# Reciprocal roots of latent and token-block norms taken by GpSimd's power in place of eleven small VectorE operations

## The chip, the cores and the metric

The kernel is one program on one core of a Trainium2 chip. Its engines are TensorE (PE, matrix products; PEld is its loading of the stationary operand), VectorE (DVE), ScalarE (ACT), GpSimd (POOL) and SyncE (SP, which issues the transfers). Each engine works through its own instructions in program order and waits at an instruction until what that instruction needs is there. The metric is device time in microseconds (us).

## The reference, cut to what matters

Two layers of a hybrid encoder over 1024 tokens of width 1024, in f32. Each layer has a token mixer of four head groups (a convolution module, a gated linear recurrence, a short gated convolution and latent attention), then cross-attention into 256 memory tokens, then a SwiGLU feed-forward part. The change touches the latent attention alone:

```python
def rms_norm(x, g):
    y = x * lax.rsqrt(jnp.mean(x * x, axis=-1, keepdims=True) + EPS)
    return y * g

def mla(ud, cos, sin, qa_g, wuq, kva_g, wukv, qn_g, kn_g):
    cq, ckv, kr = jnp.split(ud, [256, 384], axis=-1)
    q  = (rms_norm(cq, qa_g) @ wuq).reshape(b, s, 4, 96)
    kv = (rms_norm(ckv, kva_g) @ wukv).reshape(b, s, 4, 128)
    k_nope, v = jnp.split(kv, [64], axis=-1)
    k = concatenate([k_nope, broadcast_to(kr, (b, s, 4, 32))], axis=-1)
    q, k = rms_norm(q, qn_g), rms_norm(k, kn_g)
    # rotary on the last 32 of 96 columns of q and k
    return blocked_attention(q, k, v)
```

So every token has two latent norms (`cq` of 256, `ckv` of 128 columns) and eight head norms (four of `q`, four of `k`, 96 columns each), and each needs a reciprocal square root.

## The kernel before, in words

**Products.** f32 operands are split into a high and a low part, and a product is three matmuls (high by high, high by low, low by high: `mm3`). A product of a weight tile with 512 tokens is 24 matmuls, `pd<-n,wh` twice for each `pd<-n,wl`, where `n` is the normed input in 128-row pieces, and `wh`, `wl` are the parts of a weight that arrives by DMA as `wr`, is copied by ACT (L136) and has its remainder taken by DVE or POOL (L137). Results stand in three kinds of PSUM buffers, two of each: `pd`, the "t" kind (`cs`, `ukv`, `uq`, `rb`), and one for scores.

**Latent attention.** `mla_proj` makes the three latent pieces `ch`, `cl` (high and low part) and their squares `sqv`, `sqq`. `mla_stats` (once for each latent norm) sums the squares of the eight token blocks with TensorE (`cs<-ones,sq`, 128x1 each), multiplies twice by the norm of the layer's input (`xr`), takes the reciprocal roots of eight columns and leaves them in `rqkv`. `mla_prep` works on a pair of token blocks of 128, so four calls a layer. For each block it makes `ukv` (three matmuls of 512 columns), evicts keys and values by ACT, takes the low part `V` by DVE (L659), sums the squares of the keys (L662), then makes `uq` (six matmuls of 384 columns), copies it and sums its squares (L669). Of the pair's sixteen sums `hss` it takes the reciprocal roots `hr`; these scale `tok`, the queries and keys (L685 and L686 on DVE, L687 on POOL), and the rotary part follows on DVE and POOL (L696 to L698).

`ukv`, `uq`, `cs` and the transposes `hT` of the keys share the two "t" buffers. TensorE can make the `uq` of a block only when the buffer of the `ukv` before it is free, and that is after L659.

**The roots.** `rsqrt_cols` scales and adds epsilon (L147, `ra`). It then has two ways. Without the flag, POOL raises to the power -0.5 in one operation (L149):

```python
        if not act:
            nc.gpsimd.tensor_tensor(out=out, in0=a, in1=self.nhalf[:, :n], op=ALU.pow)
            return
```

With the flag, DVE takes a first guess by a shift and a subtraction on the bits (L152, L153) and makes three Newton steps of three operations (L155 to L157): eleven operations, each on `n` columns.

**Order.** The mixer (`block`) calls its parts by a written list of tokens, `ORDER`; `mt` is `mla_stats`, `pr` is `mla_prep`, `mp` the latent products, `cx`, `ct` and `sb` the short convolution (`cpad`, `yc`, `gc`), `hk` and `hh` the transposes of keys and queries, `S` the first scores. `PRIO` gives some of them a head start, `pr.0` one of 1200. A scheduler then places the instructions of each engine by these and by its own estimates of durations, so another operation in `rsqrt_cols` also changes where its neighbours stand.

The part of the list around the change, once per layer:

```
uk ih.1.0 mp.0 kr mp.2 po.0 nd po.1 mt.0 mp.1 rg mt.1 pr.0 fl.0
cx.0 pr.1 cx.1 ct.1 ct.0 fl.1 sb.0 hk.0.0 pr.2 pr.3 sb.1 hk.0.1 hh.0.0 hh.0.1 S.0
```

Of the kernel before, what the change touches and what calls it, by code (L numbers as in the profile page):

```python
# [79 lines left out]
class Trunk:  # L80
# [542 lines left out]
    def mla_stats(self, i, sq, rq):  # L623
        nc = self.nc
        p = self.pt("cs")
        for b in range(8):
            self.mm(p[:, b:b + 1], sq[i][:, b * 128:(b + 1) * 128], self.ones[:, 0:1])
        a = self.st("rqa")
        rr = rq[:, 8 * i:8 * i + 8]
        for hf in range(2):  # L630
            r1, o = self.r1[hf][:, :4], hf * 4
            nc.vector.tensor_tensor(out=a[:, o:o + 4], in0=p[:, o:o + 4], in1=r1, op=ALU.mult)
            nc.vector.tensor_tensor(out=a[:, o:o + 4], in0=a[:, o:o + 4], in1=r1, op=ALU.mult)
        self.rsqrt_cols(a[:, :8], 8, (128, 256)[i], rr, True)
        for hf in range(2):
            o = hf * 4
            nc.vector.tensor_tensor(out=rr[:, o:o + 4], in0=rr[:, o:o + 4], in1=self.r1[hf][:, :4], op=ALU.mult)

    def mla_prep(self, B0, cq, rq, ks, rt, wuq, wukv, tok, V):
        nc = self.nc  # L640
        tok += [self.m4("tok") for _ in range(2)]
        V.append(self.m4("V", F32R))
        i96 = 96 ** -0.5
        ss = self.st("hss")
        ssv = ss[:, :16].rearrange("p (b j) -> p b j", b=2)
        for b in range(2):
            B = B0 + b
            o = B * 128
            q4 = tok[B][:, 0:384].rearrange("p (h e) -> p h e", h=4)
            k4 = tok[B][:, 384:768].rearrange("p (h e) -> p h e", h=4)  # L650
            p2 = self.pt("ukv")
            self.mm3(p2, [(cq[2][0][:, o:o + 128], cq[2][1][:, o:o + 128], wukv[0][:, :512], wukv[1][:, :512])])
            rk = rq[:, B:B + 1]
            pk = p2[:, :256].rearrange("p (h e) -> p h e", h=4)
            nc.scalar.activation(out=k4[:, :, 0:64], in_=pk, func=AF.Identity, scale=rk)
            Vv = V[B // 2][:, (B % 2) * 512:(B % 2) * 512 + 512].rearrange("p (h j e) -> p h j e", h=4, j=2)
            pv = p2[:, 256:512].rearrange("p (h e) -> p h e", h=4)
            nc.scalar.activation(out=Vv[:, :, 0, :], in_=pv, func=AF.Identity, scale=rk)
            nc.vector.scalar_tensor_tensor(out=Vv[:, :, 1, :], in0=pv, scalar=rk, in1=Vv[:, :, 0, :].bitcast(F32), op0=ALU.mult, op1=ALU.subtract)  # L659
            s = self.t2("hk")  # L660
            nc.scalar.activation(out=s[:, :256].rearrange("p (h e) -> p h e", h=4), in_=k4[:, :, 0:64], func=AF.Square, scale=i96)
            nc.vector.tensor_reduce(out=ssv[:, b, 4:8], in_=s[:, :256].rearrange("p (h e) -> p h e", h=4), op=ALU.add, axis=AX.X)  # L662
            p = self.pt("uq")
            self.mm3(p[:, :384], [(cq[k][0][:, o:o + 128], cq[k][1][:, o:o + 128],
                                   wuq[0][:, k * 384:(k + 1) * 384], wuq[1][:, k * 384:(k + 1) * 384]) for k in range(2)])
            nc.scalar.copy(out=tok[B][:, 0:384], in_=p[:, :384])
            s = self.t2("hq")
            nc.scalar.activation(out=s[:, :384], in_=tok[B][:, 0:384], func=AF.Square, scale=i96)
            nc.vector.tensor_reduce(out=ssv[:, b, 0:4], in_=s[:, :384].rearrange("p (h e) -> p h e", h=4), op=ALU.add, axis=AX.X)  # L669
        nc.vector.tensor_tensor(out=ssv[:, :, 4:8], in0=ssv[:, :, 4:8], in1=ks[:, B0:B0 + 2].unsqueeze(2).to_broadcast([128, 2, 4]), op=ALU.add)  # L670
        rqb = rq[:, 8 + B0:10 + B0].unsqueeze(2).to_broadcast([128, 2, 4])
        for _ in range(2):
            nc.vector.tensor_tensor(out=ssv[:, :, 0:4], in0=ssv[:, :, 0:4], in1=rqb, op=ALU.mult)
        r = self.st("hr")
        self.rsqrt_cols(ss[:, :16], 16, 1, r[:, :16], True)
        rv = r[:, :16].rearrange("p (b j) -> p b j", b=2)
        nc.vector.tensor_tensor(out=rv[:, :, 0:4], in0=rv[:, :, 0:4], in1=rqb, op=ALU.mult)
        for b in range(2):
            self.mla_rope(B0 + b, tok, rv[:, b, :], rt)
# [815 lines left out]
```

## Time and profile before

| | |
|---|---|
| timed, median of 3 | 2930.03 us (2922.39 to 2930.04) |
| profiled execution | 2921.93 us, span 2920.2 us, mean granted clock 0.974 |
| TensorE | 2769.6 us busy, 14520 matmuls |
| VectorE | 1844.2 us busy, 2793 instructions |
| GpSimd | 1266.6 us busy, 845 instructions |
| ScalarE | 1095.2 us busy, 1826 instructions |

The span is the time from the first instruction to the last on the profiled core; the profiled execution's own time is 1.7 us more. A timeline line gives the start and the duration of one instruction (or a run of equal ones, xcount), its engine, line and tiles (out<-in, without the numbers of the tiles); the bracket at its end is the idle time of that engine just before it and the instruction that ended it. DVE operations overlap their neighbours a little, so starts can be closer together than durations.

### The profile page before, as it was taken

To read this page: it belongs to the slowest core of one execution; us is meant where nothing else is said; L and a number is where in the kernel's file an instruction comes from. 1 tells how busy PE (TensorE), PEld (TensorE's weight loads), DVE (VectorE), ACT (ScalarE), POOL (GpSimd) and SP (SyncE) were. 2 spreads that over 40 slices of the span, in tenths; PEclk is the share of its full clock that TensorE was granted. 3 is DMA by queue.
4 is the path that set the end of the run, shared out by engine and by line. 5 is a ranking of instruction groups with operands and counts; after the bars stand their busy time and mean duration, and the time that the engine had idled before them with its cause. 6 is when DMAs were issued, how large, how long until landed. Compare 5 with 4: busy or idle time off the path is not lost.

```text
span 2920.2 us, 37768 instructions
## 1 busy us (share of the span) xinstructions
PE 2769.6 (95%) x14520; PEld 2299.1 (79%) x14520; DVE 1844.2 (63%) x2793; ACT 1095.2 (38%) x1826; POOL 1266.6 (43%) x845
## 2 busy tenths in 40 slices
PE   8979999998899999999999899999998999999999
PEld 6868878887678888777878687788776788887877
DVE  7986778576745555553359767785766455556332
ACT  5314427454532222431233244274554322224111
POOL 4122214242467777434331232242334687774422
PEclk9989999998999999999999999999989999999999
DMA  4200111230212222434221001112202222224423
GB/s 143 67 28 26 44 54 35 94 94 15 84 56 85 87 87 87 141 128 136 73 101 42 17 26 51 56 57 76 80 25 84 65 87 79 75 85 163 129 76 101
DMA packets 85572, 222.00 MB, mean 76 GB/s; under 512 B 9744, under 2 KB 9872, under 8 KB 85392
## 3 DMA queue, kind: packets, MB, share of 16 engines
q1 hardware_dynamic: 84240, 215.40, 23.1%
q0 software_dynamic: 1152, 4.19, 0.5%
q8 instruction: 114, 1.87, 0.3%
q14 instruction: 66, 0.54, 0.1%
HBM read 173.42 MB, written 46.14 MB: 75 GB/s over the span
## 4 chain that ended last, share of the span: by engine, by line
PE 67%; DVE 14%; issue 7%; POOL 5%; ACT 4%; DMA 2%; SPq 0%; DVEq 0%; POOLq 0%; ACTq 0%
PE pd L119 29%; PE X L119 7%; PE Q L119 7%; PE R L119 7%; PE Y L119 4%; DVE cacc L545 3%; PE pv L119 2%; PE S L119 2%; PE PT L749 2%; PE lv L119 1%; DMA hr<-h_scr 1%; PE cs L119 1%; PE rb L119 1%; DVE n L808 1%; DVE AT L410 1%
## 5 line engine op out<-in xcount | busy, mean ns | idle before, releaser
L119 PE MATMUL pd<-n,wh 128*128 128x512 f32 x2880 | 927.2, 401 | 27.6 <-ACT wh L136 9.6
L119 PEld LDWEIGHTS pd<-n,wh 128*128 128x128 f32 x2880 | 546.0, 192 | 150.7 <-ACT wh L136 11.3
L119 PE MATMUL pd<-n,wl 128*128 128x512 f32 x1440 | 575.1, 400 | 4.5 <-POOL wl L137 4.5
L137 POOL TENSOR_TENSOR wl<-wr,wh 128x1024 fp32r<-128x1024 f32 x86 | 208.8, 2429 | 359.5 <-ACT wh L136 355.2
L136 ACT CAST wh<-wr 128x1024 fp32r<-128x1024 f32 (+2 forms) x146 | 150.8, 1035 | 478.7 <-PE pd L119 412.6
L119 PEld LDWEIGHTS pd<-n,wl 128*128 128x128 f32 x1440 | 276.2, 192 | 65.1 <-POOL wl L137 5.8
L789 DVE TENSOR_TENSOR y<-y,pd 128x512 f32<-128x512 f32 x160 | 109.5, 685 | 244.3 <-PE pd L119 244.1
L770 POOL TENSOR_SCALAR P<-P,rsum 128x256 f32<-128x256 f32 (+1 forms) x128 | 109.0, 860 | 199.3 <-DVE rsum L768 163.6
L119 PE MATMUL X<-n,wh 128*128 128x512 f32 x608 | 187.3, 389 | 0.0
L1213 POOL TENSOR_TENSOR wl<-wq,wh 128x1024 fp32r<-128x1024 f32 x60 | 159.3, 2666 | 49.4 <-ACT wh L1212 49.4
L545 DVE SCALAR_TENSOR_TENSOR cacc<-hpad,cols,cacc 128x1009 f32<-128x1009 f32 (+14 forms) x120 | 168.9, 1443 | 0.5
L1213 POOL TENSOR_TENSOR wl<-wr,wh 128x1024 fp32r<-128x1024 f32 x54 | 145.1, 2698 | 45.6 <-ACT wh L1212 45.6
L1212 ACT CAST wh<-wq 128x1024 fp32r<-128x1024 f32 x60 | 63.2, 1053 | 235.0 <-issue 123.7
L416 POOL TENSOR_TENSOR K<-K,F 128x512 f32<-128x512 f32 x56 | 86.2, 1546 | 132.2 <-DVE F L418 119.8
L1212 ACT CAST wh<-wr 128x1024 fp32r<-128x1024 f32 x54 | 56.9, 1054 | 226.4 <-issue 126.3
L119 PE MATMUL pd<-hh,wh 128*128 128x512 f32 x320 | 127.9, 400 | 11.4 <-DVE y L789 6.3
L119 PEld LDWEIGHTS X<-n,wh 128*128 128x128 f32 x608 | 114.1, 188 | 23.7
L119 PE MATMUL pd<-hh,wl 128*128 128x512 f32 x320 | 126.2, 394 | 0.0
L119 PE MATMUL pd<-hl,wh 128*128 128x512 f32 x320 | 125.9, 393 | 0.0
L814 POOL TENSOR_TENSOR acc<-acc,xsq 128x512 f32<-128x512 f32 x48 | 73.2, 1525 | 110.6 <-ACT xsq L812 83.9
L119 PE MATMUL X<-n,wl 128*128 128x512 f32 x304 | 118.3, 389 | 0.0
L119 PE MATMUL S<-n,n 96*128 96x512 f32 x384 | 111.0, 410 | 2.7 <-ACT P L766 2.5
(377 smaller groups left out, 6279.0 us busy)
## 6 DMA issues: line engine op xcount, KB each, us to landing
wr<-in_w_dram SPq DMA_DIRECT2D x48, 512.0 KB, 4.1
wr<-in_w2b_dram SPq DMA_DIRECT2D x48, 512.0 KB, 3.6
wq<-in_w_dram SPq DMA_DIRECT2D x40, 512.0 KB, 4.2
hr<-h_scr SPq DMA_DIRECT2D x80, 256.0 KB, 3.8
wr<-in_w_in_dram SPq DMA_DIRECT2D x38, 512.0 KB, 3.5
wr<-in_w_out_dram SPq DMA_DIRECT2D x24, 512.0 KB, 3.5
h_scr<-h SPq DMA_DIRECT2D x38, 256.0 KB, 4.4
h_scr<-u SPq DMA_DIRECT2D x38, 256.0 KB, 4.1
```

Source lines behind the costliest of these rows:

```text
L119: self.nc.tensor.matmul(out, lhsT, rhs, start=start, stop=stop, skip_group_check=onto)
L136: nc.scalar.copy(out=hi[:, :F], in_=raw[:, :F])
L137: self.lo_eng.tensor_tensor(out=lo[:, :F], in0=raw[:, :F], in1=hi[:, :F].bitcast(F32), op=ALU.subtract)
L410: nc.vector.copy_predicated(out=H["AT"][u][:, :1024].rearrange("p (b t) -> p b t", b=8), data=p[:, :].rearrange("p (b t) -> p b t", b=8), ...
L416: nc.gpsimd.tensor_tensor(out=ka, in0=ka, in1=apx(f, HT + m, [[2 * m, nb], [-HT - m, 2], [0, m]]), op=ALU.mult)
L545: self.nc.vector.scalar_tensor_tensor(out=dst[:, o:e], in0=src[:, o + d:e + d], scalar=w, in1=dst[:, o:e], op0=ALU.mult, op1=ALU.add)
L749: nc.tensor.transpose(out=p[:, j * 128:(j + 1) * 128], in_=P[:, o:o + 128], identity=self.ident)
L770: nc.gpsimd.tensor_scalar(out=P[:, i * n:(i + 1) * n], in0=P[:, i * n:(i + 1) * n], scalar1=ri[:, i:i + 1], scalar2=1.0, op0=ALU.mult, op1 ...
L789: self.nc.vector.tensor_tensor(out=x, in0=x, in1=p, op=ALU.add)
L814: (nc.vector if m % 2 == 0 else nc.gpsimd).tensor_tensor(out=a, in0=a, in1=q, op=ALU.add)
L1212: nc.scalar.copy(out=hi, in_=src)
L1213: self.lo_eng.tensor_tensor(out=lo, in0=src, in1=hi.bitcast(F32), op=ALU.subtract)
```

## The change

The last argument of two calls of `rsqrt_cols` goes, so the call in `mla_stats` (128x8, two per layer) and the one in `mla_prep` (128x16, four per layer) take the power on POOL. That is 12 calls; each loses eleven DVE operations and gains one POOL operation. The calls in `hgrn_post` and `head_norm` keep the flag. The lists `ORDER` and `PRIO` are as before.

```diff
@@ mla_stats
-        self.rsqrt_cols(a[:, :8], 8, (128, 256)[i], rr, True)
+        self.rsqrt_cols(a[:, :8], 8, (128, 256)[i], rr)
@@ mla_prep
         r = self.st("hr")
-        self.rsqrt_cols(ss[:, :16], 16, 1, r[:, :16], True)
+        self.rsqrt_cols(ss[:, :16], 16, 1, r[:, :16])
         rv = r[:, :16].rearrange("p (b j) -> p b j", b=2)
```

The scheduler's placement changes in two stretches, one per layer, on TensorE and DVE and in two places on ACT; outside them the order of every engine is the same, and SyncE's is the same throughout.

TensorE in the first layer, at the second sums of squares (`mt.1`) and the first `ukv` (`pr.0`), before; `n_96` is the first piece of the normed input in the product `pd_3081`, so six of its matmuls stand ahead of the sums `cs`:

```order
L119 MATMUL pd_3081<-n_96,wl_3072 128x512
L119 MATMUL pd_3081<-n_102,wh_3071 128x512
L119 MATMUL pd_3081<-n_103,wh_3071 128x512
L119 MATMUL pd_3081<-n_102,wl_3072 128x512
L119 MATMUL cs_2938<-ones,sqq_2609 128x1
L119 MATMUL ukv_2973<-wh_2587,ch_384_2677 128x512
```

The same place now; `pd_3045` is the same product, `n_126` its fifth piece and `n_134` its sixth:

```order
L119 MATMUL pd_2888<-n_303,wl_2855 128x512
L119 MATMUL pd_3045<-n_126,wh_3035 128x512
L119 MATMUL pd_3045<-n_127,wh_3035 128x512
L119 MATMUL pd_3045<-n_126,wl_3036 128x512
L119 MATMUL pd_3045<-n_134,wh_3035 128x512
L119 MATMUL cs_2926<-ones,sqq_2609 128x1
L119 MATMUL ukv_2949<-wh_2587,ch_384_2677 128x512
```

Sixteen matmuls of the product stand ahead of the sums now, and it begins inside the product before it (`pd_2888`).

DVE in the first layer, third pair of token blocks (`pr.2`), before; `V_3573` (L659) belongs to the next block, of the fourth pair, and `yc` to the short convolution:

```order
L147 TENSOR_SCALAR ra_3535<-hss_3488 128x16
L152 TENSOR_SCALAR rt_3538<-ra_3535 128x16
L659 SCALAR_TENSOR_TENSOR V_3573<-ukv_3575,rqkv_191,V_3573 128x4x64
L153 TENSOR_SCALAR ry_3537<-rt_3538 128x16
L601 TENSOR_TENSOR yc_2332<-yc_2332,pd_3423 128x512
L155 TENSOR_TENSOR rt_3538<-ry_3537 128x16
L156 SCALAR_TENSOR_TENSOR rt_3538<-rt_3538,ra_3535 128x16
L157 SCALAR_TENSOR_TENSOR ry_3537<-rt_3538,ry_3537 128x16
```

The same place now, from L147 on:

```order
L147 TENSOR_SCALAR ra_3487<-hss_3440 128x16
L677 TENSOR_TENSOR hr_3486<-hr_3486,rqkv_191 128x2x4
L686 TENSOR_TENSOR tok_3437<-tok_3437,hr_3486 128x4x64
L685 TENSOR_TENSOR tok_3437<-tok_3437,hr_3486 128x384
L685 TENSOR_TENSOR tok_3438<-tok_3438,hr_3486 128x384
L696 TENSOR_TENSOR rp_3494<-tok_3437,sqv_2608 128x128 x2
L686 TENSOR_TENSOR tok_3438<-tok_3438,hr_3486 128x4x64
L697 TENSOR_TENSOR tok_3437<-rp_3494 128x8x16
L698 TENSOR_TENSOR tok_3437<-rp_3494 128x8x16
L696 TENSOR_TENSOR rp_3504<-tok_3438,sqv_2608 128x128 x2
L659 SCALAR_TENSOR_TENSOR V_3513<-ukv_3515,rqkv_191,V_3513 128x4x64
```

L677, the first reader of the roots, stands directly behind L147, as it does in all eight calls of `mla_prep`, and the next block's L659 stands behind the pair's last L696.

TensorE just ahead of the first `uq` of the fourth pair, which follows that `ukv`, before; `pd_3423` and `pd_3449` are the two halves of a product of the short convolution:

```order
L119 MATMUL pd_3423<-n_150,wh_3419 128x512
L119 MATMUL pd_3423<-n_151,wh_3419 128x512
L119 MATMUL pd_3423<-n_150,wl_3420 128x512
L119 MATMUL pd_3449<-n_249,wh_3419 128x512
L119 MATMUL uq_3585<-uqh_1393,ch_376_2610 128x384
```

The same place now; `pd_3401` is that second half:

```order
L119 MATMUL pd_3401<-n_263,wl_3372 128x512
L119 MATMUL pd_3401<-n_271,wh_3371 128x512
L119 MATMUL pd_3401<-n_272,wh_3371 128x512
L119 MATMUL pd_3401<-n_271,wl_3372 128x512
L119 MATMUL pd_3401<-n_279,wh_3371 128x512
L119 MATMUL uq_3525<-uqh_1393,ch_376_2610 128x384
```

Of the second half one matmul stood ahead of that `uq`, now thirteen, so twelve more.

## Rows read from the trace of the kernel before

**Rows 1.** Page, parts 1 and 4: busy time and share; chain that ended last

```profile
PE 2769.6 (95%) x14520; PEld 2299.1 (79%) x14520; DVE 1844.2 (63%) x2793; ACT 1095.2 (38%) x1826; POOL 1266.6 (43%) x845
...
PE 67%; DVE 14%; issue 7%; POOL 5%; ACT 4%; DMA 2%; SPq 0%; DVEq 0%; POOLq 0%; ACTq 0%
```

**Rows 2.** Windows: stretch, length, busy PE, PEld, DVE, ACT, POOL, clock, DMA, GB/s

```profile
345.00:450.00 105.00, 101.44 (x484) 82.58 (x483) 78.80 (x222) 35.45 (x67) 24.98 (x34) 1.00 0.16 56
1795.00:1900.00 105.00, 101.49 (x486) 82.68 (x484) 78.45 (x222) 35.36 (x67) 24.67 (x34) 1.00 0.17 56
```

**Rows 3.** Timeline of DVE, first pair's roots, first layer

```profile
367.43 0.17 DVE L147 TENSOR_SCALAR ra<-hss 128x16 f32<-128x16 f32 x1
...
369.94 0.17 DVE L677 TENSOR_TENSOR hr<-hr,rqkv 128x8 f32<-128x8 f32 x1
```

**Rows 4.** Timelines of POOL and DVE, power operations elsewhere and what stands beside them

```profile
1291.52 0.71 POOL L149 TENSOR_TENSOR gr<-ra,nhalf 128x2 f32<-128x2 f32 x1
...
1671.66 1.02 POOL L149 TENSOR_TENSOR lr<-ra,nhalf 128x4 f32<-128x4 f32 x1 [26.83 <-DVE ra L147]
...
1671.42 0.16 DVE L147 TENSOR_SCALAR ra<-cs 128x4 f32<-128x4 f32 x1 [3.13 <-PE cs L119]
...
1508.57 1.94 POOL L149 TENSOR_TENSOR xr<-ra,nhalf 128x4 f32<-128x4 f32 x1 [7.85 <-DVE ra L147]
...
1508.41 1.23 DVE L137 TENSOR_TENSOR wl<-wr,wh 128x1024 fp32r<-128x1024 f32 x1
```

**Rows 5.** Chain that ended last, first layer, product matmuls

```profile
346.20 10.79 PE pd L119 x47
```

**Rows 6.** Timelines of ACT, DVE and TensorE, first pair of the first layer

```profile
350.22 0.60 ACT L616 ACTIVATE csq<-pd 128x512 f32<-128x512 f32 x1 [2.98 <-PE pd L119]
...
352.60 0.75 DVE L618 SCALAR_TENSOR_TENSOR cl<-pd,cols,ch 128x512 fp32r<-128x512 f32 x1
...
365.77 0.55 DVE L669 TENSOR_REDUCE hss<-hq 128x4 f32<-128x384 f32 x1
...
367.03 0.37 DVE L673 TENSOR_TENSOR hss<-hss,rqkv 128x8 f32<-128x8 f32 x2
...
374.87 0.50 PE L119 MATMUL ukv<-wh,ch 128*128 128x512 f32 x1 [1.04 <-DVE V L659]
```

**Rows 7.** Timelines of TensorE and DVE, second pair

```profile
398.05 0.73 PE L119 MATMUL pd<-n,wh 128*128 128x512 f32 x2 [0.86 <-DVE cpad L590]
...
399.44 0.80 DVE L543 TENSOR_SCALAR yc<-cpad,cols 128x1024 f32<-128x1024 f32 x1
```

**Rows 8.** Timelines of DVE and TensorE, third and fourth pair

```profile
423.46 0.17 DVE L147 TENSOR_SCALAR ra<-hss 128x16 f32<-128x16 f32 x1
...
423.76 0.48 DVE L659 SCALAR_TENSOR_TENSOR V<-ukv,rqkv,V 128x256 fp32r<-128x256 f32 x1
...
426.70 0.17 DVE L677 TENSOR_TENSOR hr<-hr,rqkv 128x8 f32<-128x8 f32 x1
...
430.70 0.48 DVE L696 TENSOR_TENSOR rp<-tok,sqv 128x128 f32<-128x128 f32 x2
...
424.29 0.44 PE L119 MATMUL uq<-uqh,ch 128*128 128x384 f32 x1 [0.35 <-DVE V L659]
...
432.97 0.41 PE L119 MATMUL uq<-uqh,ch 128*128 128x384 f32 x1 [1.31 <-DVE V L659]
```

**Rows 9.** Timelines of DVE and TensorE, start of the attention

```profile
445.20 0.69 DVE L186 TENSOR_TENSOR nacc<-nacc,nsq 128x512 f32<-128x512 f32 x1 [0.30 <-ACT nsq L185]
...
446.04 1.02 PE L119 MATMUL cs<-ones,nacc 128*128 128x1 f32 x8
```

**Rows 10.** Windows around an idle stretch of TensorE in the second layer

```profile
1581.30:1585.40 4.10, 0.00 (x0) 0.00 (x0) 4.10 (x3) 1.02 (x3) 4.02 (x3) 1.00 0.00 0
1585.40:1588.80 3.40, 3.28 (x15) 3.28 (x16) 3.40 (x3) 0.43 (x2) 1.95 (x3) 0.50 0.02 5
```

## The prediction

> **What bounds the kernel now.** I read the busy shares and the shares of the chain that ended last first: TensorE is busy 95% of the span and holds 67% of the chain, VectorE (DVE) 63% and 14%, GpSimd (POOL) 43% and 5% [rows 1]. So DVE time is worth something only where TensorE stands still for DVE. The twelve calls that change lie in two stretches of 105 us, one per layer, and their busy times by window agree to 0.4 us [rows 2]; I work on the first and double it. TensorE is busy 101.4 of 105 us there [rows 2]: all that could be won is 3.6 us a layer, 7.2 us in all, a quarter of a per cent. Then I read the timelines of DVE and TensorE in that stretch for what each idle piece waited for, the order of both programs for what stands there afterwards, and last the lone power operations elsewhere in the trace.
>
> **What goes and what comes.** Each call loses eleven DVE operations. In one on 16 columns L147 starts at 367.43, takes 0.17, and L677, which needs the roots, starts at 369.94 [rows 3]: 2.34 us from the end of L147. Twelve calls make some 28 us of DVE work; off the chain it is worth nothing. What comes is one power operation on POOL per call, 128x8 in four (mla_stats) and 128x16 in eight (mla_prep). The trace has it on 2 and 4 columns only. With DVE idle beside it, 128x2 took 0.71 and 128x4 1.02 us; POOL starts 0.08 us after the end of L147 (1671.42 + 0.16, then 1671.66) [rows 4]. Two columns cost 0.31, so 0.157 a column and 0.39 fixed: an estimate of 1.65 us for 8 columns and 2.9 us for 16. With the same 0.08 back to DVE, L677 would come 3.08 us after L147 ends in place of 2.34: **+0.75 us in each of the eight**. The lower bound is a time that does not grow with columns, 1.02 us, the upper one the slowest power on 4 columns, 1.94 us beside a large DVE operation [rows 4], that is 0.9 more than alone, so 3.8 us. I take 2.9, since in the new order DVE has nothing else to do meanwhile.
>
> That last point is the heart of it. DVE works in its order, and in the new order L677 stands directly behind L147 in all eight: DVE does not get 2.3 us of freedom, it stands still for 3.1. In mla_stats the first L637 likewise waits for 1.65 + 0.16 = 1.8 us; that is less than the eleven operations take there, but the roots are not late today. POOL itself is idle before each of these (its next work, L687, waits for the same roots), so nothing queues behind the power there.
>
> The Trainium skill, GPSIMD Engine Reference, section "Elementwise — side-by-side cycle accounting", measures about 2.6 cycles per element for a two-input tensor_tensor at 1.2 GHz. By that 14 more columns than 2 are 0.03 us and the power on 16 takes 0.74 us, less than the eleven operations. The trace disagrees for power: two columns cost 0.31 us [rows 4], seventy times that rule's price.
>
> **What moves, walked through the first layer.** A product matmul of 512 columns follows the next in 10.79 / 47 = 0.23 us [rows 5].
>
> (a) First pair of token blocks. In the new order ten more product matmuls stand ahead of the column sums and the ukv matmuls (16 of that product instead of 6): 2.3 us later for everything behind them. That product is also begun inside the one before it, after 12 of its 24 matmuls. The product before that ended at 350.2 (the square L616 starts then), so this place is reached near 352.9; its buffer comes free with L618 at 353.35 [rows 6]: 0.5 us of new idle time. Today 0.71 us pass between the end of the last reduction L669 (366.32) and L673 (367.03) [rows 6], filled by operations of mla_stats; now about 0.4 of it stays, as DVE stands still once for the power of mla_stats. So the roots come 2.3 + 0.5 - 0.3 + 0.75 = 3.2 us later, and with them L659, for which TensorE waits 1.04 us at 374.87 today [rows 6]. The matmuls put ahead are no longer there to fill in afterwards: TensorE reaches that wait only 0.5 us later than now and idles some 3.8 us. **+3.2.**
>
> (b) Second pair. TensorE waits 0.86 us for L590, at the end of a DVE chain that runs through the roots [rows 7]: +0.75. L543, 0.80 us [rows 7], now stands ahead of the weight remainder L137 that TensorE needs next; two matmuls moved there fill 0.45 of it: +0.3. **+1.0.**
>
> (c) Third and fourth pair. Today L659 of the next block stands directly behind L147 (423.46, then 423.76), and the uq matmuls wait for it only 0.35 us [rows 8]. In the new order L659 stands behind the whole rotary part, after the last L696 of the pair, which today starts at 430.70 and takes 0.48 for its two operations. L677 itself does not move (today two other operations stand among the eleven, so it comes at 426.70; now 423.63 + 3.08 = 426.7) [rows 8]. So L659 ends near 431.6. TensorE has 12 product matmuls moved ahead of uq, 2.7 us, and is done with them at 423.9 + 2.7 = 426.7: it idles 4.9 us. Then uq 1.05 us, its copy and three matmuls, ukv at 433.3, L659 of that near 435.5; eight matmuls cover it, uq at 435.9 to 436.9, one matmul more, 437.1. Today the last uq starts at 432.97 after 1.31 us of waiting [rows 8] and all this ends at 434.0. **+3.1.**
>
> (d) Start of the attention. The fourth pair's roots come 0.75 us later; the sums of L186 that TensorE reads at 446.04 are ready at 445.9 today [rows 9]. **+0.7.**
>
> One layer is 3.2 + 1.0 + 3.1 + 0.7 = 8.0, two are 16.0 us.
>
> (e) The clock. Idle stretches of TensorE of 4.1 us cost more than themselves here: after the one from 1581 to 1585 the granted clock of the next 3.4 us is 0.50, the lower of its two levels (1.2 GHz), after full clock before, while the waits of 1.04 and 1.31 us of this stretch leave it at 1.00 [rows 2, 10]. At half pace 3.4 us of dense matmuls lose 1.6 us (TensorE is the bound right after these waits, so nothing hides it). Two waits of about 4 to 5 us per layer, (a) and (c), make 4 x 1.6 = 6.4 us.
>
> **The sum** is 16.0 + 6.4 = 22.4 us. The profiled execution took 2921.93 us (span 2920.2), near the fastest of the three timed runs (2922.39) and 8.1 below their median 2930.03. I add it to the middle of the profiled time and the median, 2926: **2948 us**.
>
> **Rivals.** *A, the power does not grow with its columns* (the skill's rule above goes this way): 1.02 us on 16 as on 4. Then L677 comes 1.18 us after L147, 1.9 earlier than in my walk each time: (a) 3.2 - 1.9 and 0.6 off for mla_stats, +0.7; (b) the 0.86 wait goes, the 0.3 stays, -0.5; (c) L659 ends near 429.7, +1.2; (d) 0. That is 1.4 a layer, 2.8 in all, no long idle stretch, and 2926 + 3 = 2929: no change. For it: POOL's plain operations are cheap per column; against it: 0.31 us for two columns. The moved matmuls keep even this from being a gain. It decides if the power on 16 columns stays under about 1.7 us. *B, the clock does not fall*: other work of TensorE around the waits is dense and 1.0 to 1.3 us left it alone; against: the 4.1 us stretch. Sum 16, 2942: still slower. *C, power on 16 columns at 3.8 us*, by a port shared with what DVE does: 0.9 more in (a), (b), (c) and (d), 3.6 a layer, 7 in all, 2955. For it the 1.94 on 4 columns; against: DVE stands still. *D, a real gain*: the freed DVE work shows where the attention starts. Against: it is at most the 7.2 us of idle time in the two stretches.
>
> **How the numbers follow.** Forecast 0.58, A 0.15, B 0.17, C 0.06, D 0.04. About 0.3% (8.8 us) is what a measurement of this kernel can tell from no change. The forecast, C and most of B are beyond it, A is within, D at its edge: faster 0.05, same 0.16, slower 0.79. The range goes from 2930 (B from the fastest timed run, with a power somewhat quicker than the estimate) to 2962 (C, or the forecast with a second fall of the clock per layer, from the median); A lies below it and is what is left out.
>
> **What would show it.** In the profile after: power on 128x16 at 2.5 to 3.3 us; DVE idle before L677 and ended by POOL, about 3 us in eight places; TensorE's wait for L659 before ukv near 3.8 us and before uq near 4.9 us, once each per layer, and the second wait before uq gone; granted clock 0.50 behind them; TensorE busy still about 101 of some 115 us in each stretch; the rest of the span unchanged. Wrong if the power on 16 columns is near 1 us, if L659 is ready long before its matmuls, or if the time lost lies outside these two stretches.

## The result, and the profile after

The changed kernel takes 2949.89 us (median of 5, 2946.12 to 2951.19) against 2930.03 (median of 5, 2922.39 to 2934.44) for the kernel before in the same comparison: a ratio of 1.0087, 95% interval 1.0065 to 1.0108, so 19 to 32 us slower. The ratio is estimated from all the runs and is not the quotient of the two medians, which would be 1.0068. The forecast was 2948. A second comparison gave 2948.62 against 2923.21, 1.0093 (1.0073 to 1.0113).

The profiled execution took 2947.69 us, span 2945.9, 25.7 us more than before. To see where, take two instructions that no kernel here moves: ACT's first square of the query latent's second piece in a layer (L616, 350.22 in [rows 6]) and the first power of the attention's norms, which ends the stretch (L149, `gr`). These are their rows before, columns as in the other timelines (the first layer's L616 is in [rows 6]):

```profile
1800.16 0.60 ACT L616 ACTIVATE csq<-pd 128x512 f32<-128x512 f32 x1 [3.23 <-PE pd L119]
...
447.34 1.02 POOL L149 TENSOR_TENSOR gr<-ra,nhalf 128x4 f32<-128x4 f32 x1 [4.19 <-DVE ra L147]
...
1897.27 1.02 POOL L149 TENSOR_TENSOR gr<-ra,nhalf 128x4 f32<-128x4 f32 x1 [4.19 <-DVE ra L147]
```

and the four of them after:

```profile
350.22 0.60 ACT L616 ACTIVATE csq<-pd 128x512 f32<-128x512 f32 x1 [3.27 <-PE pd L119]
...
459.58 1.01 POOL L149 TENSOR_TENSOR gr<-ra,nhalf 128x4 f32<-128x4 f32 x1 [4.79 <-DVE ra L147]
...
1815.28 0.60 ACT L616 ACTIVATE csq<-pd 128x512 f32<-128x512 f32 x1 [3.00 <-PE pd L119]
...
1925.09 1.01 POOL L149 TENSOR_TENSOR gr<-ra,nhalf 128x4 f32<-128x4 f32 x1 [4.79 <-DVE ra L147]
```

Before, a stretch takes 447.34 - 350.22 = 97.1 us in either layer, 194.2 in both; after, 109.4 and 109.8, 219.2 in both. The two stretches lose 24.9 of the 25.7 us. I call this sum of two the stretch sum; it is the measure of the experiments below, as a timed run moves by several us with TensorE's clock elsewhere.

The busy times of the page answer to [rows 1]: DVE worked 20 us less, POOL 30 more, and TensorE's share of the chain fell from 67 to 64%.

```profile
PE 2779.8 (94%) x14520; PEld 2306.1 (78%) x14520; DVE 1824.5 (62%) x2661; ACT 1095.5 (37%) x1826; POOL 1296.3 (44%) x857
...
PE 64%; DVE 15%; issue 9%; POOL 6%; ACT 4%; DMA 3%; SPq 0%; POOLq 0%; DVEq 0%; ACTq 0%
```

The listing of line L149 (duration in ns, least/median/greatest) has the new operations and who waited for them (us in total, times):

```profile
L149 POOL TENSOR_TENSOR hr<-ra,nhalf x8: 2898/2899/2901, 370.1 to 1913.6; 128x16 f32<-128x16 f32 x8
...
L149 POOL TENSOR_TENSOR rqkv<-ra,nhalf x4: 1647/1648/1649, 353.5 to 1830.9; 128x8 f32<-128x8 f32 x4
...
  DVE hr L677: 24.1, 8
```

2.90 and 1.65 us are what the 2 and 4 columns of [rows 4] led to, and DVE stands still for 3.0 us in each of the eight. On DVE's timeline, first pair and then third, beside [rows 3] and [rows 8]:

```profile
369.83 0.17 DVE L147 TENSOR_SCALAR ra<-hss 128x16 f32<-128x16 f32 x1
373.02 0.17 DVE L677 TENSOR_TENSOR hr<-hr,rqkv 128x8 f32<-128x8 f32 x1 [3.01 <-POOL hr L149]
...
429.38 0.17 DVE L147 TENSOR_SCALAR ra<-hss 128x16 f32<-128x16 f32 x1
432.57 0.17 DVE L677 TENSOR_TENSOR hr<-hr,rqkv 128x8 f32<-128x8 f32 x1 [3.01 <-POOL hr L149]
...
436.95 0.47 DVE L659 SCALAR_TENSOR_TENSOR V<-ukv,rqkv,V 128x256 fp32r<-128x256 f32 x1
```

L659 of the next block comes 7.6 us after L147; in [rows 8] it came 0.3 us after it. TensorE's timeline shows what that does, beside [rows 6 to 9]: two long waits for L659 (3.23 and 4.87 us), three of 0.78, 0.81 and 0.31 us in the second pair where there was one of 0.86, and one of 0.77 at the start of the attention.

```profile
377.93 0.80 PE L119 MATMUL ukv<-wh,ch 128*128 128x512 f32 x1 [3.23 <-DVE V L659]
...
402.04 0.70 PE L119 MATMUL pd<-n,wh 128*128 128x512 f32 x2 [0.78 <-DVE gc L584]
403.55 0.73 PE L119 MATMUL pd<-n,wh 128*128 128x512 f32 x2 [0.81 <-DVE cpad L590]
405.54 0.50 PE L119 MATMUL pd<-n,wl 128*128 128x512 f32 x1 [0.31 <-DVE wl L137]
...
437.48 0.69 PE L119 MATMUL uq<-uqh,ch 128*128 128x384 f32 x1 [4.87 <-DVE V L659]
...
458.27 1.02 PE L119 MATMUL cs<-ones,nacc 128*128 128x1 f32 x8 [0.77 <-DVE nacc L186]
```

And the windows around the two long waits, columns as in [rows 2], show the granted clock (third from the end; 1.00 is TensorE's full speed) falling behind each:

```profile
374.00:378.00 4.00, 0.77 (x5) 0.45 (x4) 4.00 (x12) 0.48 (x1) 2.14 (x4) 0.99 0.17 66
378.00:382.00 4.00, 4.00 (x13) 3.54 (x14) 2.05 (x5) 1.32 (x3) 0.00 (x0) 0.59 0.00 0
382.00:386.00 4.00, 4.00 (x23) 3.23 (x22) 0.69 (x1) 1.38 (x2) 0.00 (x0) 1.00 0.19 70
...
436.00:440.00 4.00, 2.52 (x8) 2.43 (x9) 2.75 (x9) 0.20 (x1) 0.27 (x1) 0.50 0.00 0
440.00:444.00 4.00, 4.00 (x13) 3.20 (x12) 1.32 (x3) 1.95 (x5) 0.00 (x0) 0.66 0.00 0
```

In four us at full clock TensorE does 23 matmuls, in the four behind a wait 13.

### The profile page after: what moved, and what is told of

Same layout as the page of the kernel before. It is cut to its first block, busy times and chain, and to the rows that moved or that the text cites. A ratio compares the mean times of both kernels' runs of the same rounds, so it can differ in the third digit from the quotient of the medians.

```text
span 2945.9 us, 37646 instructions
## 1 busy us (share of the span) xinstructions
PE 2779.8 (94%) x14520; PEld 2306.1 (78%) x14520; DVE 1824.5 (62%) x2661; ACT 1095.5 (37%) x1826; POOL 1296.3 (44%) x857
## 4 chain that ended last, share of the span: by engine, by line
PE 64%; DVE 15%; issue 9%; POOL 6%; ACT 4%; DMA 3%; SPq 0%; POOLq 0%; DVEq 0%; ACTq 0%
PE pd L119 27%; PE X L119 7%; PE Q L119 7%; PE R L119 7%; PE Y L119 4%; DVE cacc L545 3%; PE pv L119 2%; PE S L119 2%; PE PT L749 2%; DMA hr<-h_scr 1%; PE lv L119 1%; DVE wl L137 1%; PE rb L119 1%; PE cs L119 1%; DVE n L808 1%
## 5 line engine op out<-in xcount | busy, mean ns | idle before, releaser
L137 POOL TENSOR_TENSOR wl<-wr,wh 128x1024 fp32r<-128x1024 f32 x86 | 208.6, 2428 | 358.6 <-ACT wh L136 354.3
```

The source lines that it names most:

```text
L137: self.lo_eng.tensor_tensor(out=lo[:, :F], in0=raw[:, :F], in1=hi[:, :F].bitcast(F32), op=ALU.subtract)
```

## The experiments

The theory: DVE stands still from L147 until POOL's power is done, the next L659 stands behind that and the rotary part, and TensorE waits for L659. Rivals: the new order costs by itself; the power costs by itself; the clock falls for another reason. Each row is one program; where there are several timed runs, it is compared with the kernel before run in turn with it. The ratio is estimated from all runs of both, as above.

| kernel | us (runs) | before | ratio, 95% | stretch sum |
|---|---|---|---|---|
| before, two profiles | | | | 194.2, 194.2 |
| changed, two profiles | 2949.89 (5), 2948.62 (6) | 2930.03, 2923.21 | 1.0087, 1.0093 | 219.2, 215.9 |
| product for power | 2930.29 (12) | 2920.71 | 1.0030 (1.0016 to 1.0044) | 193.4 |
| wait only | 2936.08 (11) | 2920.71 | 1.0044 (1.0030 to 1.0057) | 201.3 |
| mla_prep only | 2955.81 (6) | 2920.71 | 1.0122 (1.0102 to 1.0141) | 220.2 |
| mla_stats only | 2927.64 (11) | 2920.71 | 1.0028 (1.0013 to 1.0043) | 196.4 |
| L659 forward | 2951.70 (1) | 2921.44 | | 219.2 |
| power twice | 2977.91 (1) | 2921.44 | | 247.7 |
| rotary part later, power | 2923.61 (12) | 2921.44 | 1.0009 (0.9990 to 1.0029) | 196.9 |
| rotary part later, eleven | 2919.74 (12) | 2921.44 | 0.9993 (0.9977 to 1.0008) | 194.2 |
| waits filled | 2944.98 (6) | 2923.21 | 1.0079 (1.0055 to 1.0104) | 211.8 |
| and L596 on DVE | 2923.55 (12) | 2920.86 | 1.0009 (0.9994 to 1.0024) | 190.0 |

**Product for power.** The same order of every engine, with a short operation in the power's place, so this kernel leaves out the twelve reciprocal roots.

```diff
-            nc.gpsimd.tensor_tensor(out=out, in0=a, in1=self.nhalf[:, :n], op=ALU.pow)
+            nc.gpsimd.tensor_tensor(out=out, in0=a, in1=self.nhalf[:, :n], op=op)   # mult in the twelve calls
```

> The power of the twelve calls is replaced by a product on GpSimd of the same tiles (so the roots are left out and the output is not the reference's); the order of every engine is that of the changed kernel. Theory of the wait (VectorE stands still from L147 until GpSimd is done): a GpSimd product on 16 columns is short (one on 128 columns, L687, takes 0.49 us before), so L677 comes about 0.4 us after L147 ends in place of 3.1 in all eight calls, the waits of TensorE of 3.2 and 4.9 us per layer go below 3 us, the granted clock stays at 1.00 there, and the time falls below the kernel before by 4 to 11 us (2919 to 2926), some 25 to 30 us under the changed kernel. Rival, the new order itself costs (ten and twelve matmuls ahead, L659 behind the rotary part): it stays, and the time is within 8 us of the changed kernel's 2950.

The listing of L149 in its profile, form as above:

```profile
L149 POOL TENSOR_TENSOR hr<-ra,nhalf x8: 218/221/223, 370.3 to 1902.8; 128x16 f32<-128x16 f32 x8
...
L149 POOL TENSOR_TENSOR rqkv<-ra,nhalf x4: 201/203/206, 353.9 to 1832.2; 128x8 f32<-128x8 f32 x4
```

With 0.22 us in place of 2.90 the stretch sum is 193.4: the 25 us are gone, so the order alone costs nothing there. But it gains nothing either, where I had expected 4 to 11 us, and the time is 9.6 us above the kernel before, though the stretches are not longer. Its runs had a mean granted clock of 0.9712, those of before 0.9756 (means over 12 and 27 runs). Runs of before alone go from 2913.82 us at 0.979 to 2931.24 at 0.971, 2.2 us for each 0.001, and 4.4 times that is the 9.6: by this estimate the clock outside the stretches makes all of it. Its profile shows one such place, the same 191 matmuls in the second layer, before and here:

```profile
1640.00:1662.00 22.00, 19.18 (x191) 16.43 (x190) 16.84 (x32) 4.50 (x8) 2.43 (x2) 0.97 0.08 22
```

```profile
1647.00:1675.50 28.50, 25.75 (x191) 22.46 (x191) 16.85 (x32) 4.68 (x8) 2.43 (x2) 0.69 0.06 17
```

The order there is that of before. Why its clock is lower there is open.

**Wait only.** The order and the eleven operations of before, but the last takes its value from a power.

```diff
+            nc.gpsimd.tensor_tensor(out=root, in0=a, in1=self.nhalf[:, :n], op=ALU.pow)
...
+                nc.vector.scalar_tensor_tensor(out=out, in0=t, scalar=0.0, in1=root, op0=ALU.mult, op1=ALU.add)
```

> The kernel before in its own order, with its eleven operations, but in mla_prep the last of them takes its value from a power on GpSimd (128x16) started behind L147, so that only the wait is new. Theory of the wait: the root comes 0.75 + 0.2 = 0.9 us later in each of eight; the first and the second pair and the start of the attention pass it on (0.8 each), the third does not: 2.4 a layer, 5 us in all, 2935 against 2930 for before; no stretch of TensorE idle over 3 us and no fall of the clock. Rival, the order is what costs: the time is that of before within 2 us. Rival, the power on GpSimd slows the VectorE operations beside it: the eleven take clearly more than 2.34 us in all up to the last, and the time rises by more than 8 us.

DVE's timeline, first pair; L160 is the last of the eleven, L682 what L677 was:

```profile
366.91 0.17 DVE L147 TENSOR_SCALAR ra<-hss 128x16 f32<-128x16 f32 x1
...
370.11 0.17 DVE L160 SCALAR_TENSOR_TENSOR hr<-rt,hx 128x16 f32<-128x16 f32 x1 [0.93 <-POOL hx L152]
370.32 0.17 DVE L682 TENSOR_TENSOR hr<-hr,rqkv 128x8 f32<-128x8 f32 x1
```

The root's last operation waits 0.93 us, and the operations beside the power keep their 0.17 us: no cost of the power to small operations of DVE. In all eight calls DVE waits 5.9 us for the power, against 24.1 in the changed kernel, since the eleven operations fill the rest. The stretch sum grows by 7.1 us (5 expected, with a clock of 0.99). The time grew by more than the 5 us expected, 15.4 in the medians and 10.5 between the spans of the two profiles. That is also more than the 8 us that the rival in that expectation named; its other half, slower small operations, did not come. What exceeds the 7.1 lies outside the stretches, and its cause is not shown.

**One call or the other.** Power in mla_prep alone, then in mla_stats alone.

```diff
-        self.rsqrt_cols(a[:, :8], 8, (128, 256)[i], rr)
+        self.rsqrt_cols(a[:, :8], 8, (128, 256)[i], rr, True)
```

> Power only in mla_prep (eight calls on 16 columns), eleven operations in mla_stats. Theory of the wait: nearly the whole loss is here: two waits of TensorE per layer of about 5 us, both for L659 before uq, each followed by a stretch at granted clock 0.5 that costs 1.6 to 2.6 us: 8 a layer without the clock, 24 us in all, 2950 to 2956. Rival, the order around the first sums of squares (mla_stats) costs a large part: 2938 or less.

```diff
-        self.rsqrt_cols(ss[:, :16], 16, 1, r[:, :16])
+        self.rsqrt_cols(ss[:, :16], 16, 1, r[:, :16], True)
```

> Power only in mla_stats (four calls on 8 columns), eleven operations in mla_prep. Theory of the wait: VectorE waits 1.8 us for the power where it worked 2.3 us before; only the moved matmuls at the first pair cost, 1.6 a layer: +3 us, 2933, no idle stretch of TensorE over 3 us and clock 1.00 there. Rival, the order around the first sums of squares costs a large part of the 20 us: 2938 or more. A gain (2927 or less) would say that the freed operations were on the path.

The waits of TensorE in the first stretch with mla_prep alone (us in total, times, longest):

```profile
PE uq L119 <- DVE V L659: 9.2, 2, 4.9
```

In the stretches the eight calls on 16 columns make the whole loss, +26.0; the four on 8 columns make +2.2, near the 3 forecast. The medians rose by more, 35.1 and 6.9 us, at mean clocks of 0.9697 and 0.9735 against 0.9756.

**L659 forward, power twice.** Priority for L659; a second power ahead of the first.

```diff
+            with self.tc.high_priority(offset=5000):
                 nc.vector.scalar_tensor_tensor(out=Vv[:, :, 1, :], ...)
```

> The changed kernel with L659 given priority, which puts it directly behind L677 in the third pair in place of behind the last L696 (and takes the twelve matmuls ahead of uq back). Theory of the wait: L677 still waits for the power and L659 with it, so TensorE still waits 3 to 5 us for L659 twice per layer, and from the first pair's stretch to the attention each layer loses as much as in the changed kernel, 12 us (10 to 14). Rival, the place of L659 behind the rotary part is the loss: the waits fall below 2 us and a layer loses 7 us or less.

```diff
+            if twice:
+                nc.gpsimd.tensor_tensor(out=out, in0=a, in1=self.nhalf[:, :n], op=ALU.pow)
```

> The changed kernel with the power of mla_prep issued twice on GpSimd in each of the eight calls, so that its result comes 2.9 us later. Theory of the wait: every term that the power sets grows by 2.9 to 3 us (first pair, second pair, third and fourth, start of the attention): 12 us more per layer, 24 us more than the changed kernel over both, some 50 us above the kernel before, and TensorE's longest waits about 7 us. Rival, the power is mostly hidden or only its first use counts: less than 10 us more than the changed kernel.

TensorE's waits in the first stretch, L659 forward and then power twice (L660 and L661 are L659 there):

```profile
PE uq L119 <- DVE V L660: 7.3, 2, 4.0
```

```profile
PE uq L119 <- DVE V L661: 6.7, 1, 6.7
PE ukv L119 <- DVE V L661: 6.2, 1, 6.2
```

Directly behind L677, L659 is late all the same: 219.2. A power more adds 28.5 us to 219.2 (24 expected). Both follow the wait.

**Rotary part later.** L677 and the rotary part become a step of their own, queued on DVE behind the next pair's second L659; with the power, then with the eleven operations.

```diff
-mt.1 pr.0 fl.0 cx.0 pr.1 cx.1 ct.1 ct.0 fl.1 sb.0 hk.0.0 pr.2 pr.3 sb.1
+mt.1 vf.0 pr.0 fl.0 cx.0 vf.1 pr.1 ro.0 cx.1 ct.1 ct.0 fl.1 sb.0 vf.2 pr.2 ro.1 hk.0.0 vf.3 pr.3 ro.2 ro.3 sb.1
...
+        with self.tc.issue_after(nxt.ins):     # nxt: L659 of the next pair's second block
             nc.vector.tensor_tensor(out=rv[:, :, 0:4], in0=rv[:, :, 0:4], in1=rqb, op=ALU.mult)
             for b in range(2):
                 self.mla_rope(B0 + b, tok, rv[:, b, :], rt)
```

> The changed kernel, all twelve powers kept, but the part of mla_prep behind the roots (L677 and the rotary part) is issued as a step of its own, and its VectorE operations are queued behind the next pair's second L659. Theory of the wait: VectorE has the next pair's work between L147 and L677, so it stands still for the power only at the last pair, TensorE's two long waits for L659 go, and so does the fall of the clock behind them: some 8 us under the kernel before (2921 in the last runs), 2911 to 2918. Rival, the power itself is what costs (GpSimd busy 2.9 us at a time, a port shared with VectorE): the time stays 10 us or more above the same order with eleven operations (the next kernel).

> The same step and the same queueing, but with the eleven VectorE operations of the kernel before in all twelve calls. Theory of the wait: what decides is what stands between L147 and the next L659, so this order gains as much with eleven operations as with the power: 2909 to 2917, within 4 us of the power version. Rival, freed VectorE time is worth something once the wait is hidden: the power version is 5 us or more below this one. Rival, the power itself costs: it is 10 us or more above.

All twelve powers are still there and the loss is gone, from 25 us to 2.6 in the stretches and to no measurable difference in time from the kernel before. So what cost 25 us was not the power by itself but what stood behind it. Against the eleven operations in the same order the power is no gain: it is 2.6 us dearer in the stretches and 3.9 in the medians (6.3 in the means), and where that comes from is not shown. Neither version gains the 8 us or so that I expected. TensorE still waits 2.75 us in the power version, and its timelines of TensorE, DVE and POOL say why:

```profile
426.09 0.41 PE L119 MATMUL uq<-uqh,ch 128*128 128x384 f32 x1 [2.75 <-DVE V L661]
...
422.16 3.39 DVE L137 TENSOR_TENSOR wl<-wr,wh 128x1024 fp32r<-128x1024 f32 x1
425.47 0.47 DVE L661 SCALAR_TENSOR_TENSOR V<-ukv,rqkv,V 128x256 fp32r<-128x256 f32 x1
...
422.05 2.41 POOL L596 TENSOR_TENSOR yc<-yc,rb 128x1024 f32<-128x1024 f32 x1
```

L137, begun just behind POOL's product L596, took 3.39 us. With the eleven L137 began first and took 1.21; there L596 took 3.37 in place of 2.41, the DVE operation on 16 columns behind L137 took 2.34, and TensorE waited 2.5 us:

```profile
423.82 1.21 DVE L137 TENSOR_TENSOR wl<-wr,wh 128x1024 fp32r<-128x1024 f32 x1
424.96 2.34 DVE L156 SCALAR_TENSOR_TENSOR rt<-rt,ra 128x16 f32<-128x16 f32 x1
...
423.89 3.37 POOL L596 TENSOR_TENSOR yc<-yc,rb 128x1024 f32<-128x1024 f32 x1 [7.38 <-DVE rt L155]
```

**And L596 on DVE.**

```diff
-        self.nc.gpsimd.tensor_tensor(out=yc[:, :T], in0=yc[:, :T], in1=self.rb[:, :T], op=ALU.mult)
+        self.nc.vector.tensor_tensor(out=yc[:, :T], in0=yc[:, :T], in1=self.rb[:, :T], op=ALU.mult)
```

> The power version with the rotary part queued behind the next pair's second L659, and besides the four products L596 (yc by rb, 128x1024, 2.4 us on GpSimd) moved to VectorE, where a product of that size (L137) takes 1.22 us. Theory (the 2.7 us that TensorE waited for L659 before the fourth pair's uq in that version came from L137 on VectorE taking 3.39 in place of 1.22 us while L596 ran on GpSimd beside it): L137 takes 1.2 to 1.3 us again, that wait falls under 1 us, the granted clock stays at 1.00 behind it, and the version is 3 to 8 us faster than without this, 2912 to 2919 with the kernel before at 2922. Rival, L659 is late for another reason (VectorE's own queue, which now has 1.2 us more in it): the wait stays above 2 us and the time is that of the kernel before within 3 us or above it.

DVE's timeline and TensorE's waits in the first stretch:

```profile
424.79 1.21 DVE L596 TENSOR_TENSOR yc<-yc,rb 128x1024 f32<-128x1024 f32 x1
425.93 0.47 DVE L661 SCALAR_TENSOR_TENSOR V<-ukv,rqkv,V 128x256 fp32r<-128x256 f32 x1
...
426.92 1.21 DVE L137 TENSOR_TENSOR wl<-wr,wh 128x1024 fp32r<-128x1024 f32 x1
```

```profile
PE uq L119 <- DVE V L661: 0.7, 1, 0.7
```

The collision and the wait are gone, and the stretch sum is 190.0, 4.2 under before. The time is not, where I had expected a gain of 3 to 8 us: 2923.55, no difference to before, at a mean clock of 0.9735 against 0.9754. So this is no version that beats both kernels. The eleven operations with L596 on DVE were not run.

**Waits filled.** The changed kernel in its order, with useless matmuls in the place of the two long waits.

```diff
+        with self.tc.issue_after(behind):
+            for i in range(n):                 # 26 ahead of the ukv, 40 ahead of the uq
+                last = self.nc.tensor.matmul(o, w, x, start=i == 0, stop=i == n - 1)
```

> The changed kernel again, unaltered, beside the next one on the same chip: 2945 to 2955, mean granted clock about 0.971, the two long waits of TensorE per layer (3.2 and 4.9 us) each followed by some 4 to 8 us at granted clock 0.5 to 0.66.

> The changed kernel in the same order on every engine, with useless matmuls (256 columns, into an idle PSUM buffer) in the place of the two long waits of TensorE per layer: 26 ahead of the ukv, 40 ahead of the uq, which cover about 3 and 4.5 us; nothing reads them. Theory of the clock (the fall behind the waits is brought on by TensorE's standing still there): TensorE does 132 matmuls more and the time falls all the same, by 6 to 10 us against the changed kernel, since the stretches behind the waits keep a granted clock of 1.00; each layer's stretch loses 8 us in place of 12. Rival, the clock falls for other reasons: the time is that of the changed kernel within 3 us or above it.

> The kernel before again, unaltered, for a second profile: in the two stretches of 105 us its times agree with the first profile to 0.5 us. If the granted clock of the two profiles differs elsewhere, the difference in time lies where the clock differs (2.3 us for each 0.001 of the mean clock over the runs so far).

The windows behind the two waits now, to be held against those of the changed kernel:

```profile
378.00:382.00 4.00, 3.85 (x23) 3.33 (x22) 3.31 (x10) 1.32 (x3) 0.00 (x0) 1.00 0.00 0
...
436.00:440.00 4.00, 3.91 (x24) 3.23 (x23) 2.86 (x10) 1.00 (x2) 0.10 (x1) 1.00 0.00 0
```

The clock stays, and the stretch sum falls by 7.4 or 4.1 us against the two profiles of the changed kernel: the waits bring on the fall. In the medians it is 3.6 us less (6 runs each, 2937.82 to 2957.30 against 2943.31 to 2958.41), under the 6 to 10 expected and not clear of the spread. The second profile of before gave the same stretch sum to within 0.02 us.

## Why the prediction was right

The filled version has the waits without the clock, so the terms can be read one by one: the time between starts of the same instructions of ACT and POOL in the first layer, worked out from the three traces (us).

| from, to | before | filled | more | predicted | changed |
|---|---|---|---|---|---|
| (a) L616 to the wh at 395.36 | 45.14 | 48.25 | 3.1 | 3.2 | 49.71 |
| (b) to the wh at 414.26 | 18.90 | 20.26 | 1.4 | 1.0 | 20.24 |
| (c) to the last copy of uq, 434.29 | 20.03 | 22.99 | 3.0 | 3.1 | 25.11 |
| (d) to the gr at 447.34 | 13.05 | 14.29 | 1.2 | 0.7 | 14.30 |

- *The power*: 2.90 and 1.65 us against an estimate of 2.9 and 1.65, L677 3.0 us behind the end of L147 against 3.08. Right.
- *(a) to (d)*: 8.7 a layer against 8.0. Right, and the waits too: 3.23 and 4.87 us against 3.8 and 4.9. (a)'s wait is shorter than forecast, as TensorE came to it 0.9 us later than before and not 0.5; (b) and (d) were under-sized by 0.4 and 0.5.
- *(e) the clock*: changed less filled is 1.5 in (a) and 2.1 in (c), 3.6 a layer in one profile and 2.2 in the other (97.1 to 108.0 there, less 8.7), against 3.2 (two falls of 1.6). Right in kind; the size varies between executions.
- *Rival A* (a cheap power): ruled out by 2.90 us; where the operation was made cheap, at 0.22 us, the order gave -0.8 us over both layers (+0.5 and -1.4) against the 2.8 that I had worked out for 1.02 us. *B* is ruled out by the windows, *C* by the duration, *D* (freed DVE work shows) by the product for power and by the two versions with the rotary part later.
- *The sum and the time*: 22.4 us against 24.9 in the stretches, of one profile, and 21.7, of the other. That the forecast of 2948 lies within 2 us of the measured time is in part luck: the base of 2926 was 4 us under the 2930.03 of its comparison, and the medians there are only 19.9 apart; in the second comparison the base was 2.8 too high and the medians are 25.4 apart.
- *The rest of the span unchanged*: 0.8 us, as said. It doesn't hold for every kernel here: those with the new steps, and the product for power, met a lower clock elsewhere.

The Trainium skill's rule for plain products (GPSIMD Engine Reference, section "Elementwise — side-by-side cycle accounting") does hold where it was meant: the product on 16 columns took 0.221 us and on 8 columns 0.203, and the page's 2.6 cycles per element at 1.2 GHz make, as an estimate, 0.017 of that difference of 0.018. It is power that costs some seventy times as much per column: 0.157 us against 0.0022.

## What to carry to other kernels

A shorter list of instructions is not a shorter path: before moving work to another engine, look at what will stand between the producer and the first reader on the waiting engine, and at what is queued behind that reader. If nothing stands between them, the engine gets the other's latency as idle time, and an instruction that never needed the result is late with it. Give the waiting engine other work first (here the rotary part behind the next pair's L659), and price an operation by its own rows at two sizes, as here 2 and 4 columns gave the 16, not by a relative that looks alike.

## What the runs showed that I had not expected

DVE and POOL hold each other up in large products, which here read two tiles from SBUF. L137 took 3.39 us beside L596 and 1.21 without; where L137 came first, L596 took 3.37 in place of 2.41, and a DVE operation on 16 columns behind it 2.34 in place of 0.16. The Trainium skill has this (GPSIMD Engine Reference, section "Specifications": the SBUF interfaces are shared with VectorE, with contention for DVE instructions with two SBUF inputs), and the trace agrees for the products. The power showed it one way only: small DVE operations with two inputs kept their 0.17 us beside it, but it was itself longer beside a large DVE operation, 1.94 us on 4 columns in [rows 4] and 3.48 in place of 2.90 in the second pair of the power version with the rotary part later.

Of the variants with many timed runs none had so high a mean clock as the kernel before (0.9753 over its runs in turn with them; 0.9697 to 0.9747 for the others, the highest not clear of it), also where the order elsewhere is the same. At 2.2 us for 0.001 that decides differences of a few us, and its cause stays open.
